# Order of the split products in a two-layer encoder: x low first, and the low weight part right behind the high one for half of each page

## The chip, the cores and the metric

The kernel runs on one core of one Trainium2 chip. The metric is the device time of the whole program in microseconds, the median of several runs. PE is TensorE, DVE is VectorE, ACT is ScalarE, POOL is GpSimd, SP is the engine that issues most loads.

## The reference

Two layers over 256 tokens of width 4096. Each layer normalises x, makes one combined input projection (4096 x 11264), runs an attention branch and a retention branch on its columns, gates both, and adds the output projection (4096 x 4096) of their concatenation to x. A last normalisation follows.

```python
for l in range(DEPTH):                       # 2
    h = rmsnorm(x, norm_w[l])
    proj = h @ w_in[l]                       # (256, 4096) @ (4096, 11264)
    aq, ak, av, ag, rq, rk, rv, rg = jnp.split(proj, SPLIT_POINTS, axis=-1)
    a_out = silu(ag) * gqa_attention(rope(norm(aq)), rope(norm(ak)), av)
    r_out = silu(rg) * rmsnorm(bidirectional_retention(rope(rq), rope(rk), rv), ret_norm[l])
    x = x + concat([a_out, r_out]) @ w_out[l]     # (256, 4096) @ (4096, 4096)
return rmsnorm(x, final_norm)
```

Everything is float32, and nearly all the work lies in the two projections.

## The kernel before

**Blocks and pairs.** Each projection is a phase (four in all: in, out, in, out). A phase runs over blocks of 1024 output columns (11 blocks for the input projection, 4 for the output one), and a block over 16 pairs of 128-row pieces of the inner dimension. For each pair the two halves of the tokens and the two pieces of rows make a 2 x 2 product of blocks, and the kernel computes it by fewer products than the eight of the plain way: seven for the pairs in `SEVEN_IN` or `SEVEN_OUT` (through sums of blocks), eight for the others. Each product adds into one of seven PSUM banks M1 to M7. At the end of a block `combining` adds the banks into two pages of SBUF, `ca` and `cb`.

**Pages.** The weights come as pages of 128 x 1024 (tile `wraw`, six buffers). A page is used by some products, its `uses`: an eight-product pair has two pages of four uses, a seven-product pair has three pages of two uses, two of them sums of weight blocks (`wsum`), and one with a single use (a half page, `whb` and `wlb`).

**High and low parts.** A product of float32 values is made of three matmuls on rounded parts (type fp32r): high weight by high x, high weight by low x, low weight by high x. The x part (128 x 128) is the stationary operand, the weight part (128 x 512) the moving one. The parts of x lie in SBUF for a whole phase (`x7h`, `x7l`, `x8h`, `x8l`, `xmh`, `xml`). The parts of a weight page are made as it comes: ACT casts it to `whi` (four buffers), DVE subtracts for `wlo` (three buffers). For the "far" pages ACT makes both `fhi` and minus `fhi` in `flo`, and a DMA from POOL's queue adds the weights to `flo`. Four pairs (`DIRECT`) of the first block use the plain float32 data (part "D").

**The order of the work around the change.** In `block` (line 1516) a list `units` is written: for each page its "H" units (two matmuls with the high weight) and "L" units (one matmul with the low weight). Before, all H units of a page come first, then all its L units. The pages of the last pair (15) are sorted by bank instead, each use as H and then L. The pages `PAGE_E` of the very last block go to the end (`rest_units`). PE runs the units in exactly this order, each waiting for its data.

**The planner.** While the program is written, `run` (line 851) keeps clocks of PE, ACT and DVE with assumed costs, and hands each engine its next instruction when that clock says it would be free: the weight casts and subtractions (`Weights.high`, `Weights.low`), the splitting of x for the next phase (`split_pair`), and the steps of attention and retention, whose small matmuls (`product`, line 1114, into the bank `ps`) are put between the units. So the orders on ACT, DVE and PE depend on when the planner believes a unit can start. A page's buffers are given back when its last unit has been written (`Weights.release`).

Of the kernel before, what the change touches and what calls it, by code (L numbers as in the profile page):

```python
# [183 lines left out]
def pages_in_order(phase, first=False, last=False):  # L184
    late = [_p for _p in range(NP - 1) if _p not in SEVENS[phase]][-LATE_PAIRS:] if last else []
    skip = DIRECT if first else ()
    order = []
    for _g in groups_of(SEVENS[phase]):
        if _g[0] in skip:
            order += [(_p, _k) for _p in _g for _k in (PAGE_A, PAGE_B)]  # L190
        else:
            order += pages_of([_p for _p in _g], first and _g[0] == 0)
    for _p, _k in order:
        if _p in SEVENS[phase] and _p not in skip:
            yield _p, _k, [(_b, (ALL, _a), _h) for _b, _a, _pg, _h in SEVEN_PRODUCTS if _pg == _k]
        else:
            yield _p, _k, [
                (_b, (_i, _a), _h)
                for _b, _i, _a, _pg, _h in EIGHT_PRODUCTS
                if _pg == _k and not (_p in late and _b == "M4")  # L200
            ]
    for _p in late:
        yield _p, PAGE_E, [("M4", (_i, 1), _i) for _i in range(2)]
# [119 lines left out]
def hybrid_encoder(  # L323
# [43 lines left out]
    def t(pool, shape, tag, bufs=None, dt=F32):  # L367
        kw = {} if bufs is None else {"bufs": bufs}
        return pool.tile(shape, dt, tag=tag, name=tag, **kw)

    def f32(v):
        return v.bitcast(F32)
# [672 lines left out]
    bank = [False, 0.0]  # L1045
# [64 lines left out]
    def matmul(out, a, b, start, stop, passes=1):  # L1110
        nc.tensor.matmul(out, a, b, start=start, stop=stop)  # L1111
        pe.until = max(pe.until, now.t) + MM[math.prod(out.shape[1:])] * passes
# [7 lines left out]
    def at(parts, *index):  # L1120
        return [v[index] for v in parts]
# [391 lines left out]

    bank_at = dict.fromkeys(BANKS, 0.0)

    def block(after_pair, phase, first_order=False, order=LAST_ORDER, last=None):

        phase_now[0] = phase
        units = []
        tail, rest_units = [], []
        for p, k, uses in pages_in_order(phase, first_order, last is not None):
            if k == PAGE_E:
                rest_units += [(p, k, use, "H") for use in uses] + [(p, k, use, "L") for use in uses]
                continue
            if first_order and (p, k) == (DIRECT[0], PAGE_A):  # L1530
                uses = uses[1:] + uses[:1]
            if first_order and p in DIRECT:
                units += [(p, k, use, "D") for use in uses]
                continue
            if p == NP - 1:
                tail += [(p, k, use) for use in uses]
                continue
            units += [(p, k, use, "H") for use in uses] + [(p, k, use, "L") for use in uses]
        tail.sort(key=lambda v: order.index(v[2][0]))
        for v in tail:  # L1540
            units += [v + ("H",), v + ("L",)]
        units += rest_units
        first = {b: next(i for i, v in enumerate(units) if v[2][0] == b) for b in BANKS}
        final = {b: max(i for i, v in enumerate(units) if v[2][0] == b) for b in BANKS}
        left, uses = {}, {}
        for p, k, _, _ in units:
            left[p] = left.get(p, 0) + 1
            uses[p, k] = uses.get((p, k), 0) + 1
        acc, pages, c, fin = {}, {}, Columns(), {}
        done = []  # L1550
        urgent.append(Lane((last or combining)(acc, fin, c, order)))
        for n, (p, k, (bank, index, h), part) in enumerate(units):
            if n == len(units) - COMBINE_LEAD:
                wanted[0] = 2
            while (p, k) not in pages:
                g = weights.pages[weights.at]
                weights.at += 1
                assert g.phase == phase
                pages[g.pair, g.kind] = g
            g = pages[p, k]  # L1560

            def ready():
                if part == "D":
                    return (
                        weights.has(g, "raw")
                        and p in plain
                        and plain[p][2 if index[1] == 2 else 1] <= now.t
                        and (n != first[bank] or bank_at[bank] is not None and bank_at[bank] <= now.t)
                    )
                when = g.high_at if part == "H" else g.low_at  # L1570
                if when is None or not (when() if callable(when) else when <= now.t) or version[p] != phase or operand_at[p] > now.t:
                    return False
                return n != first[bank] or (bank_at[bank] is not None and bank_at[bank] <= now.t)

            yield ready
            if n == first[bank]:
                acc[bank] = t(pm, [P, NB], bank)
                bank_at[bank] = None
            if part == "D":
                a = None  # L1580
            elif g.seven:
                a = at(operand[p], *index, ALL)
            else:
                a = at(operand[p], ALL, 4 + index[0] if index[1] == 2 else 2 * index[0] + index[1], ALL)
            if part == "D":
                matmul(acc[bank], plain[p][0][index], f32(g.raw[0])[:, h], n == first[bank], n == final[bank], 4)
            elif part == "H":
                b = g.hi if k == PAGE_B and g.seven else g.hi[:, h]
                matmul(acc[bank], a[0], b, n == first[bank], False)
                matmul(acc[bank], a[1], b, False, False)  # L1590
            else:
                b = g.lo if k == PAGE_B and g.seven else g.lo[:, h]
                matmul(acc[bank], a[0], b, False, n == final[bank])
            if n == final[bank]:
                fin[bank] = pe.done
            uses[p, k] -= 1
            if not uses[p, k]:
                weights.release(g)
            left[p] -= 1
            if not left[p]:  # L1600
                done.append(p)
                if part == "D":
                    plain_left.remove(p)
            while done and all(not left[q] for q in range(min(done))):
                q = min(done)
                done.remove(q)
                after_pair(q)
        return c
# [181 lines left out]
    def program():  # L1790
        nonlocal sums
        for l, L in enumerate(layers):
            for bi, (one, _) in enumerate(BLOCKS):
                if bi == N_IN - 1:
                    turning.append(Turn(2 * l + 1))
                c = yield from block(turn_over, 2 * l, l == 0 and bi == 0)

                if bi == N_IN - 2:
# [45 lines left out]
            for n in range(N_OUT2):  # L1844
                final = n == N_OUT2 - 1
                if last_layer and final:

                    def after(p):
                        if p == LATE_PAIR:
                            for i in range(2):  # L1850
                                for m in range(MT):
                                    tag = "x8h" if m else "x8l"
                                    r = f32(t(ap, [P, 6, P], tag, EIGHT_ALWAYS, F32R))
                                    rest[i, m] = r[:, :4].rearrange("p k s -> p (k s)")
                                    rest["at"] = dma("sync", rest[i, m], residual(l, N_OUT - 2 + i, m))
                            for i in range(2):
                                r = f32(t(ap, [P, 6, P], ("x8h", "x8l")[i], EIGHT_ALWAYS, F32R))
                                fn.append(r[:, :4].rearrange("p k s -> p (k s)"))
                                dma("sync", fn[i], final_norm[columns(N_OUT - 2 + i)].partition_broadcast(P))

                    yield from block(after, 2 * l + 1, order=FINAL_ORDER, last=last_combining)
                else:
                    if final:
                        turning.append(Turn(2 * l + 2))
                    c = yield from block(turn_over, 2 * l + 1)
                    task(out_tasks(l, n, c), lambda c=c: c.done, need=4, own=2, hurry=n > 1, due=need_at.get((2 * l + 2, 4 * n + 1), 2e9) - DUE_LEAD)
# [70 lines left out]
```

## Time and profile before

| | us |
|---|---|
| three runs | 2621.02, 2621.44, 2623.92 |
| median | 2621.44 |
| the profiled execution's own time | 2623.02 |
| its span | 2621.2 |
| mean granted clock of PE over the span | 0.995 |

Of the span, PE is busy 99%, the loads of its stationary operand 81%, DVE 89%, ACT 73%, POOL 17%. A row of a group in the profile has the line, the engine, the operation, output and inputs by name (so `M<-whi,x8h` is a product into a bank M from the moving `whi` and the stationary `x8h`), the shapes, the count, then busy time and the mean duration of one, then the engine's idle time just before and what ended it. A timeline row has start and duration in us ahead of the same names; `[0.78 <-DVE wlb]` is idle time before it and what ended it. A row of the list of waits reads: who waited for whom, us in total, how many times, the longest one.

### The profile page before, as it was taken

The page shows a single profiled execution, that of the slowest core. Times are in us where ns is not written, and L with a number is a line of the kernel's source. Part 1 is how long each engine was busy: PE and PEld are TensorE (multiplying, and loading weights), DVE is VectorE, ACT ScalarE, POOL GpSimd, SP SyncE. Part 2 cuts the span into 40 slices and gives each one's busy share as a digit, 9 for nine tenths or more (in the row PEclk, how much of TensorE's full clock was granted, in tenths as well). Part 3 has the DMA queues.
Part 4 walks back from the last instruction along what each step waited for, and adds up shares of the span by engine and source line. Part 5 has one row for each costly group of instructions (what it writes and reads, how often), then busy time and mean ns, then how long its engine had stood idle before and what let it go on. Part 6 is the DMA issues. An engine that isn't in the chain of part 4 may idle for free.

```text
span 2621.2 us, 34650 instructions
## 1 busy us (share of the span) xinstructions
PE 2582.6 (99%) x11570; PEld 2124.0 (81%) x11570; DVE 2323.9 (89%) x2908; ACT 1910.0 (73%) x2672; POOL 436.2 (17%) x592
## 2 busy tenths in 40 slices
PE   9999999999999999999999999999999999999997
PEld 5788888888888888788788888888888888877886
DVE  7898988998888889888998889989989888997888
ACT  8777776777767688666877776767768676886665
POOL 0112211221211110221111211212212121101110
PEclk9999999999999999999999999999999999999999
DMA  9999999998898898999999999989989988989997
GB/s 298 309 296 284 273 285 281 272 300 265 279 281 267 282 272 247 296 281 279 309 270 281 287 277 290 276 267 299 282 263 283 279 263 281 283 243 273 268 275 237
DMA packets 214227, 729.62 MB, mean 278 GB/s; under 512 B 25760, under 2 KB 32544, under 8 KB 214048
## 3 DMA queue, kind: packets, MB, share of 16 engines
q1 hardware_dynamic: 149200, 523.44, 56.7%
q0 software_dynamic: 64848, 203.98, 34.3%
q8 instruction: 90, 1.47, 0.2%
q14 instruction: 89, 0.73, 0.1%
HBM read 679.08 MB, written 48.23 MB: 277 GB/s over the span
## 4 chain that ended last, share of the span: by engine, by line
PE 80%; DVE 7%; issue 4%; DMA 4%; ACT 2%; POOL 1%; SPq 0%; DVEq 0%; ACTq 0%; POOLq 0%
PE M L1111 77%; DVE wlo L232 3%; PE ps L1111 3%; DMA wraw<-in_w_in 1%; DVE wsum L232 1%; DMA pT<-p_dram 1%; ACT whi L232 1%; DMA flo<-in_w_in 1%; DVE cb L232 1%; DMA q<-q_dram 0%; DVE ca L232 0%; ACT fhi L232 0%; DMA q_dram<-cb 0%; DVE x8l L232 0%; DVE wlb L232 0%
## 5 line engine op out<-in xcount | busy, mean ns | idle before, releaser
L232 ACT CAST whi<-wraw 128x1024 fp32r<-128x1024 f32 x525 | 547.0, 1048 | 203.8 <-PE M L1111 172.8
L232 DVE TENSOR_TENSOR wlo<-wraw,whi 128x1024 fp32r<-128x1024 f32 x525 | 636.2, 1220 | 51.7 <-ACT whi L232 24.9
L232 DVE TENSOR_TENSOR wlo<-wsum,whi 128x1024 fp32r<-128x1024 f32 x432 | 526.2, 1218 | 116.7 <-PE M L1111 111.7
L232 ACT CAST whi<-wsum 128x1024 fp32r<-128x1024 f32 x432 | 453.2, 1049 | 142.4 <-PE M L1111 125.8
L1111 PE MATMUL M<-whi,x7h 128*128 128x512 f32 x1248 | 487.8, 391 | 0.0
L1111 PE MATMUL M<-whi,x7l 128*128 128x512 f32 x1248 | 486.2, 390 | 0.0
L1111 PE MATMUL M<-whi,x8h 128*128 128x512 f32 x1060 | 415.7, 392 | 6.2 <-DVE ca L232 3.1
L1111 PE MATMUL M<-whi,x8l 128*128 128x512 f32 x1060 | 414.5, 391 | 0.0
L1111 PE MATMUL M<-wlo,x7h 128*128 128x512 f32 x1248 | 386.4, 390 | 0.7 <-DVE wlo L232 0.7
L1111 PE MATMUL M<-fhi,x8h 128*128 128x512 f32 x844 | 328.8, 390 | 0.0
L1111 PE MATMUL M<-fhi,x8l 128*128 128x512 f32 x844 | 328.8, 390 | 0.0
L232 ACT CAST fhi<-wraw 128x1024 fp32r<-128x1024 f32 x215 | 226.0, 1051 | 136.6 <-PE M L1111 103.0
L1111 PE MATMUL M<-wlo,x8h 128*128 128x512 f32 x1060 | 315.9, 394 | 4.3 <-DVE wlo L232 4.1
L348 POOL DMA_DIRECT2D flo<-in_w_in x157 | 140.9, 897 | 1057.1 <-ACT flo L232 969.0
L232 DVE TENSOR_TENSOR wsum<-wraw 128x1024 f32<-128x1024 f32 x216 | 263.1, 1218 | 14.7 <-DMA wraw<-in_w_in 11.9
L1111 PEld LDWEIGHTS M<-whi,x7h 128*128 128x128 f32 x1248 | 234.9, 188 | 48.5 <-issue 0.5
L1111 PEld LDWEIGHTS M<-whi,x7l 128*128 128x128 f32 x1248 | 234.7, 188 | 48.7 <-issue 0.5
L1111 PEld LDWEIGHTS M<-wlo,x7h 128*128 128x128 f32 x1248 | 233.2, 188 | 49.6 <-DVE wlo L232 2.3
L1111 PEld LDWEIGHTS M<-whi,x8h 128*128 128x128 f32 x1060 | 199.9, 189 | 51.3 <-DVE ca L232 6.6
L1111 PEld LDWEIGHTS M<-wlo,x8h 128*128 128x128 f32 x1060 | 200.3, 190 | 48.5 <-DVE wlo L232 7.8
L232 ACT ACTIVATE flo<-fhi 128x1024 fp32r<-128x1024 f32 x215 | 228.3, 1062 | 6.8
L1111 PEld LDWEIGHTS M<-whi,x8l 128*128 128x128 f32 x1060 | 199.9, 189 | 41.0
(257 smaller groups left out, 3762.5 us busy)
## 6 DMA issues: line engine op xcount, KB each, us to landing
wraw<-in_w_in SPq DMA_DIRECT2D x703, 512.0 KB, 5.9
wraw<-in_w_out SPq DMA_DIRECT2D x256, 512.0 KB, 6.1
flo<-in_w_in POOLq DMA_DIRECT2D x157, 512.0 KB, 8.7
flo<-in_w_out POOLq DMA_DIRECT2D x58, 512.0 KB, 8.5
full<-next_dram POOLq DMA_DIRECT2D x18, 512.0 KB, 8.8
p_dram<-room POOLq DMA_DIRECT2D x64, 128.0 KB, 4.2
pT<-p_dram POOLq DMA_DIRECT2D x16, 512.0 KB, 9.1
next_dram<-room POOLq DMA_DIRECT2D x40, 128.0 KB, 6.2
```

The source lines that it names most:

```text
L232: return call(out, *args, **kwargs)
L348: getattr(nc, name).dma_start(to, src, **kw)
L1111: nc.tensor.matmul(out, a, b, start=start, stop=stop)
```

## The change

The list of units of a page is now made by `passes_of`. For the first half of the page's uses all H units come first; then for the second half each use has its H and its L unit next to one another; then the L units of the first half follow, in reverse. With four uses: H0 H1 H2 L2 H3 L3 L1 L0; with two: H0 H1 L1 L0; with one: H L. And in an H unit the matmul with the low part of x now goes first, so that the high part of x is the stationary operand of the last matmul of H and of the L behind it.

```diff
+    def passes_of(p, k, uses):
+
+        n = len(uses) // 2
+        return [(p, k, use, "H") for use in uses[:n]] + [(p, k, use, part) for use in uses[n:] for part in "HL"] + [
+            (p, k, use, "L") for use in uses[:n][::-1]
+        ]
+
...
             if k == PAGE_E:
-                rest_units += [(p, k, use, "H") for use in uses] + [(p, k, use, "L") for use in uses]
+                rest_units += passes_of(p, k, uses)
...
-            units += [(p, k, use, "H") for use in uses] + [(p, k, use, "L") for use in uses]
+            units += passes_of(p, k, uses)
         tail.sort(key=lambda v: order.index(v[2][0]))
-        for v in tail:
-            units += [v + ("H",), v + ("L",)]
+        for p, k, use in tail:
+            units += passes_of(p, k, [use])
...
             elif part == "H":
                 b = g.hi if k == PAGE_B and g.seven else g.hi[:, h]
-                matmul(acc[bank], a[0], b, n == first[bank], False)
-                matmul(acc[bank], a[1], b, False, False)
+                matmul(acc[bank], a[1], b, n == first[bank], False)
+                matmul(acc[bank], a[0], b, False, False)
```

The number of matmuls, their operands and the banks they add into are the same in both kernels; so are the loads, casts and subtractions.

## The prediction

> **What bounds the kernel now.** I read the page's first two parts, then the matmul groups of its fifth part, then a stretch of the timeline, because a busy share says nothing about how densely the matmuls follow one another.
>
> ```profile
> span 2621.2 us, 34650 instructions
> PE 2582.6 (99%) x11570; PEld 2124.0 (81%) x11570; DVE 2323.9 (89%) x2908; ACT 1910.0 (73%) x2672; POOL 436.2 (17%) x592
> ...
> L1111 PE MATMUL M<-whi,x8h 128*128 128x512 f32 x1060 | 415.7, 392 | 6.2 <-DVE ca L232 3.1
> L1111 PE MATMUL M<-wlo,x8h 128*128 128x512 f32 x1060 | 315.9, 394 | 4.3 <-DVE wlo L232 4.1
> ```
>
> PE is the bound, DVE is second. Every matmul record has its own weight-load record (11570 of each). A record of 392 ns is longer than its place in the stream, since records overlap; the distance between starts is what counts. Here are the last products of a block (pair 15), where a use runs high with x high, high with x low, low with x high:
>
> ```profile
> 1566.63 0.39 PE L1111 MATMUL M<-wlo,x8h 128*128 128x512 f32 x1
> 1566.86 0.39 PE L1111 MATMUL M<-whi,x8h 128*128 128x512 f32 x1
> 1567.09 0.39 PE L1111 MATMUL M<-whi,x8l 128*128 128x512 f32 x1
> 1567.31 0.39 PE L1111 MATMUL M<-wlo,x8h 128*128 128x512 f32 x1
> 1567.54 0.39 PE L1111 MATMUL M<-whi,x8h 128*128 128x512 f32 x1
> 1567.77 0.39 PE L1111 MATMUL M<-whi,x8l 128*128 128x512 f32 x1
> ...
> 1567.31 0.39 PE L1111 MATMUL M<-wlo,x8h 128*128 128x512 f32 x1
> 1567.32 0.19 PEld L1111 LDWEIGHTS M<-whi,x8h 128*128 128x128 f32 x1
> 1567.54 0.39 PE L1111 MATMUL M<-whi,x8h 128*128 128x512 f32 x1
> ```
>
> Starts are 0.22 to 0.23 us apart (0.227 on the mean: 1566.63 to 1567.77 is 1.14 us for five), and a load of 0.19 us starts with the matmul before it and is over before its own starts. The changed kernel has 10,776 products of this kind, as before; 10,776 x 0.227 = 2446 us, 93% of the span, is a floor that no order of products changes unless the distance itself changes. What is left for a reordering are the waits of PE:
>
> ```profile
> PE M L1111 <- DVE wlo L232: 4.8, 3, 3.4
> PE ps L1111 <- DVE pTl L232: 3.2, 6, 0.7
> PE M L1111 <- DVE ca L232: 3.1, 5, 1.0
> PE ps L1111 <- DVE aql L232: 2.5, 5, 0.7
> PE M L1111 <- DMA wraw<-in_w_in: 1.9, 1, 1.9
> PE M L1111 <- ACT whi L232: 1.8, 1, 1.8
> PE ps L1873 <- POOL whi L1870: 1.7, 1, 1.7
> PE M L1111 <- DVE wlb L232: 1.6, 3, 0.8
> ...
> PE M L1111 <- DMA flo<-in_w_in: 0.6, 1, 0.6
> PE M L1111 <- DMA flo<-in_w_out: 0.2, 1, 0.2
> ```
>
> These waits are about 20 us together, in some thirty places. So a gain of over 1% can come only from the distance.
>
> **The change, part by part.**
>
> *The same stationary operand twice in a row.* In the instruction orders of the two builds I counted neighbouring products with the very same stationary slice: 29 before, 1,992 after, so 1,963 more. No instruction goes: PE has the same number of matmuls in both. What a repeated operand is worth, this trace shows twice. The 29 pairs are in the rows above: a block's tail goes M3, M5, M4, M2, and the last use of M5 and the first of M4 both take slice 1 of pair 15. That is the step from 1567.31 to 1567.54: a load is issued all the same (1567.32) and the distance is 0.23 us. Over all 29 pairs the median distance is 227 ns, as for the other 10,652. The second place is `product` (line 1114), whose first two matmuls share a stationary operand:
>
> ```profile
> 1947.26 0.28 PE L1111 MATMUL ps<-vh,wTh 128*128 128x256 f32 x1
> 1947.38 0.28 PE L1111 MATMUL ps<-vl,wTh 128*128 128x256 f32 x1
> 1947.50 0.28 PE L1111 MATMUL ps<-vh,wTl 128*128 128x256 f32 x1
> 1947.62 0.28 PE L1111 MATMUL ps<-vh,wTh 128*128 128x256 f32 x1
> ```
>
> wTh to wTh takes 0.12 us, as do wTh to wTl and wTl to the next wTh. Value: 0. The bound on the side of a gain: two widths at 227 and 120 ns make (227 - 120) / 256 = 0.418 ns a column, so 227 - 512 x 0.418 = 13 ns a matmul that do not depend on width. Were all of that saved, 1,963 x 13 ns = 25.5 us. A loss from three accumulations in a row into one bank: the tail rows above already run whi, whi, wlo into one bank at 0.227 us, so 0.
>
> The Trainium skill ("TensorE: Matmul & The Clock Gate", section "Back-to-back issue gap") gives an isolated gap of N/2.4 + 2.5, 216 ns at 512 columns, under the 227 ns of the rows; should a repeated operand reach that gap, an estimate from that page is 1,963 x 11 ns = 22 us less. The 29 pairs do not.
>
> *The low part is needed sooner.* A page with four uses ran eight high matmuls, then four low ones. Now the first low one comes after six: its wlo (250 pages) or flo (210 pages) is needed 2 x 0.227 = 0.454 us sooner. Pages with two uses (H0 H1 L1 L0) and with one need it where they did. If every one of the 460 were just in time, that would cost 209 us. What covers it is the lead of DVE. I took every wlo's end against its first reader; of those 250 pages this is the closest:
>
> ```profile
> 2573.02 1.23 DVE L232 TENSOR_TENSOR wlo<-wraw,whi 128x1024 fp32r<-128x1024 f32 x1 [1.98 <-ACT whi L232]
> ...
> 2574.97 0.84 PE L1111 MATMUL M<-wlo,x8h 128*128 128x512 f32 x3
> ```
>
> It is ready at 2574.25, read at 2574.97: 0.72 us, over 0.454. Cost 0. The flo come by DMA, and the list of waits has two that were late already (0.6 and 0.2 us). Each grows by 0.454: +0.9 us; bounds 0 (both landings move sooner) and 1.8 (four such).
>
> *whi is released one matmul later* (its last reader is the ninth of twelve matmuls, not the eighth): ACT's next cast into that buffer can start 0.227 us later on 250 pages. PE waited for whi once in the whole run (1.8 us, near the start), so the four buffers cover it: 0; without that cover 57 us. *x low first* needs the subtraction's result one matmul sooner, a few times a phase; no wait of PE on x7l or x8l is in the list: 0.
>
> *What the planner makes of it.* It writes out the other engines' orders by its own clock, and the two builds agree but for a few places. SP and POOL keep their order. The attention and retention products stand at the same place among the main ones, except that seven groups come one matmul sooner and a few one or two later. Where a group waits for aql or pTl (11 waits above), sooner is 0.227 us more idle time: +0.4 us, bounds -0.5 and +1.6.
>
> The one place that is really rearranged is the border between the layers, near 1300 us:
>
> ```profile
> 1296.00:1303.00 7.00, 6.88 (x31) 5.36 (x29) 6.89 (x14) 6.97 (x10) 0.88 (x1) 1.00 0.68 223
> 1303.00:1310.00 7.00, 3.23 (x12) 2.06 (x12) 6.93 (x9) 5.39 (x7) 0.00 (x0) 1.00 0.75 218
> 1310.00:1314.00 4.00, 3.75 (x10) 2.98 (x11) 3.96 (x7) 2.14 (x7) 0.87 (x1) 0.57 0.82 219
> ...
> 1303.66 0.50 PE L1111 MATMUL M<-wlb,xmh 128*128 128x512 f32 x1 [0.78 <-DVE wlb L232]
> 1310.25 0.79 PE L1111 MATMUL M<-wlo,x8h 128*128 128x512 f32 x1 [3.36 <-DVE wlo L232]
> ...
> 1302.92 0.68 DVE L232 TENSOR_TENSOR wlb<-wraw,whb 128x512 fp32r<-128x512 f32 x1
> ...
> 1312.45 0.42 DVE L232 TENSOR_TENSOR x7l<-full,x7h 128x256 fp32r<-128x256 f32 x1
> 1312.78 0.82 DVE L232 TENSOR_TENSOR x7l<-xf,x7h 128x640 fp32r<-128x640 f32 x1
> ```
>
> The columns of the first three rows are the stretch, its length, and busy time of PE, PEld, DVE, ACT and POOL, then the granted clock. DVE is busy 6.9 of 7 us there and PE waits for it, so DVE's work counts in full. In the changed order the two x7l subtractions stand ahead of that wlb instead of behind the last wlo: 0.42 + 0.82 = 1.24 us more before both waits. The second wait starts later by what the first grew, so the sum is +1.24 us; bounds -5.8 (0.78 + 3.36 idle and the slow stretch behind them, 4 us at a granted 0.57, so 1.7 us, all gone) and +4 (x7l also waits for ACT's cast, and a second slow stretch follows).
>
> **Sum:** 0 + 0 + 0.9 + 0 + 0.4 + 1.24 = +2.5 us. The profiled execution took 2623.02 us (span 2621.2 and 1.8 around it) and would take 2625.5; the median of the three runs is 2621.44, 1.6 below it, so the forecast is 2624.0 us. That is +0.1%: a measurement of this kernel can tell about 0.2% (5.2 us) from no change, so I call it the same, 2616.2 to 2626.7.
>
> **The rivals.**
>
> *A repeated operand shortens the stream* (faster). The 13 ns fall away on 1,963 products: 2621.4 - 25.5 + 2.5 = 2598 us. For it: the change makes just such pairs, and 256-wide products are a thin likeness. Against it: the 29 pairs at full width, each with its own load. The Trainium skill says in the same page ("What happens when you issue a matmul") that a stationary operand may be loaded once and used repeatedly; here each matmul loads its own. Chance 0.10.
>
> *Low parts come late* (slower). Place: the 210 far pages, whose flo lands by DMA, and DVE-bound borders like the one above. Price 0.454 us a page; with the +1.6 from the other terms it decides from 8 late pages on (5.2 us). With 15 it is 6.8 + 1.6 = 8.4 us: 2630 us. For it: two flo were late already. Against it: only two of 215. Chance 0.24.
>
> *The border loses its waits*: -5.8 + 1.3 = -4.5 us, 2617 us, since ACT's and DVE's split work is spread otherwise. For it: the orders of ACT and DVE differ in many places there, and the waits are DVE's. Against it: x7l moves the wrong way. Chance 0.08, half of it below 2616.2.
>
> **Numbers.** The forecast has 0.58, of which 0.04 lies above 2626.7. Faster: 0.10 + 0.04 = 0.14. Slower: 0.24 + 0.04 = 0.28. Same: 0.54 + 0.04 = 0.58. The range runs from 2615 (the border gain, a little beyond) to 2633 (some 20 late pages): it leaves out the first rival and the far end of the second, under 2 in 10.
>
> **What would show it.** Right: the steps whi,x8h to wlo,x8h stand 0.227 us apart in the timeline, PEld has 11570 loads again, and PE's waits total a few us more, with wlb near 1304 us waiting about 2 us. Wrong: distances of 0.22 us or less at the repeated operand, or fewer loads; waits of PE on wlo or flo of some 0.4 us in many places.

## The result and the profile after

| | us |
|---|---|
| changed kernel, median of 22 runs | 2626.17 (2620.71 to 2630.55) |
| kernel before, median of 22 runs beside them | 2620.21 (2612.48 to 2624.30) |
| ratio, with its 95% interval | 1.0018 [1.001, 1.0025] |
| the profiled execution of the changed kernel | 2626.18, span 2624.4 |

By the ratio, 0.18% of 2620 us, the changed kernel takes 4.7 us longer (the means differ by 4.9 us, the medians by 6.0). That is on the edge of the 0.2% that the prediction called "the same"; the forecast was 2624.0 and the sum behind it +2.5 us. The profiled execution took 3.2 us longer than that of before (2626.18 against 2623.02).

The first rows of the page of the changed kernel, and one row of its groups:

```profile
span 2624.4 us, 34648 instructions
PE 2581.7 (98%) x11570; PEld 2123.6 (81%) x11570; DVE 2325.8 (89%) x2908; ACT 1911.0 (73%) x2672; POOL 437.2 (17%) x592
...
L1111 PE MATMUL M<-flo,x8h 128*128 128x512 f32 x844 | 262.9, 390 | 2.1 <-DMA flo<-in_w_out 1.1 <-DMA flo<-in_w_in 1.0
```

The bound is the same, and every matmul still has its own load: 11570 of each. PE is busy 0.9 us less than before and the span is 3.2 us longer, so what came in is idle time of PE or lies behind its last matmul. The list of PE's waits in the changed kernel (waiter, what it waited for, us in total, times, longest):

```profile
PE M L1111 <- DVE wlo L232: 5.4, 4, 3.3
PE ps L1111 <- DVE pTl L232: 4.0, 7, 0.9
PE ps L1111 <- DVE aql L232: 2.9, 4, 1.1
...
PE M L1111 <- DMA flo<-in_w_out: 1.1, 1, 1.1
PE M L1111 <- DMA flo<-in_w_in: 1.0, 1, 1.0
```

Over the whole list PE waited 26.1 us in 32 places, before 23.4 us in 31. The two waits for `flo` went from 0.8 to 2.1 us, those for `pTl` and `aql` from 5.7 to 6.9, those for `wlo` from 4.8 to 5.4; all others together went from 12.1 to 11.7.

The rest of the time is at the end. Here are the last rows of before that matter, from its timeline (SPq is the issue of a DMA on SP's queue):

```profile
2601.57 0.39 PE L1111 MATMUL M<-whi,x8h 128*128 128x512 f32 x1
...
2604.00 0.68 DVE L232 TENSOR_TENSOR cb<-cb,M 128x512 f32<-128x512 f32 x1
...
2604.14 0.73 PE L1111 MATMUL M<-wlo,x8h 128*128 128x512 f32 x2
...
2604.60 1.22 DVE L232 TENSOR_TENSOR wlo<-wraw,whi 128x1024 fp32r<-128x1024 f32 x1
...
2605.87 0.73 PE L1111 MATMUL M<-wlo,x8h 128*128 128x512 f32 x2
...
2607.51 0.34 SPq L348 DMA_DIRECT2D out<-ca  x1
```

The same place in the changed kernel:

```profile
2603.61 0.39 PE L1111 MATMUL M<-whi,x8l 128*128 128x512 f32 x1
...
2606.07 1.22 DVE L232 TENSOR_TENSOR wlo<-wraw,whi 128x1024 fp32r<-128x1024 f32 x1
...
2607.20 0.68 DVE L232 TENSOR_TENSOR cb<-cb,M 128x512 f32<-128x512 f32 x1
...
2607.34 0.73 PE L1111 MATMUL M<-wlo,x8h 128*128 128x512 f32 x2
...
2610.52 0.34 SPq L348 DMA_DIRECT2D out<-ca  x1
```

Before, DVE added bank M3 into `cb` and then made the last `wlo`. In the changed kernel the last `wlo` comes ahead of that addition. The addition is what the final normalisation of the first half of the tokens waits for, so the first output is issued 4.45 us after the start of the last `wlo` (2610.52 - 2606.07), not 2.91 (2607.51 - 2604.60). From the start of the last matmul (the second of the pair in the row, 2606.21 before and 2607.68 after) to the end of the span it is 15.03 us before and 16.69 after: +1.67 us. The stream ahead of it grew by 1.47 us in these two executions.

The +1.67 us is not all price, though, since the last matmul itself waits for the last `wlo`. Before, PE lost 0.30 us at 2604.14 and 0.25 us at 2605.87 to `wlo`, against starts 0.227 us apart; in the changed kernel it lost 0.10 us, at 2607.34, because each `wlo` is made one addition sooner. Counted from an earlier matmul that both kernels have at the same place (the eighteenth from the end, the first row of either block above), the first output is issued 5.94 us later before and 6.91 after: +0.97 us. The remaining 0.13 us lies between the first output and the end of the span (13.72 and 13.85 us).

### The profile page after: what moved, and what is told of

Read it like the earlier page. It is cut to its first block, busy times and chain, and to the rows that moved or that the text cites. A ratio compares the mean times of both kernels' runs of the same rounds, so it can differ in the third digit from the quotient of the medians.

```text
span 2624.4 us, 34648 instructions
## 1 busy us (share of the span) xinstructions
PE 2581.7 (98%) x11570; PEld 2123.6 (81%) x11570; DVE 2325.8 (89%) x2908; ACT 1911.0 (73%) x2672; POOL 437.2 (17%) x592
## 3 DMA queue, kind: packets, MB, share of 16 engines
q8 instruction: 90, 1.47, 0.2%
## 4 chain that ended last, share of the span: by engine, by line
PE 84%; DVE 6%; DMA 5%; issue 3%; ACT 1%; POOL 1%; SPq 0%; DVEq 0%; POOLq 0%; ACTq 0%
PE M L1111 80%; PE ps L1111 3%; DVE wlo L232 3%; DMA pT<-p_dram 1%; DVE wsum L232 1%; DMA flo<-in_w_out 1%; DMA wraw<-in_w_out 1%; DMA wraw<-in_w_in 1%; DMA q<-q_dram 1%; DVE cb L232 0%; ACT whi L232 0%; DVE pTl L232 0%; DMA flo<-in_w_in 0%; DVE wlb L232 0%; POOL rq_dram L348 0%
## 5 line engine op out<-in xcount | busy, mean ns | idle before, releaser
L1111 PE MATMUL M<-wlo,x8h 128*128 128x512 f32 x1060 | 348.6, 393 | 3.9 <-DVE wlo L232 3.9
L1111 PE MATMUL M<-flo,x8h 128*128 128x512 f32 x844 | 262.9, 390 | 2.1 <-DMA flo<-in_w_out 1.1
```

## The experiments

Each ratio is against the kernel before, run beside it on the same chip, with its 95% interval; n is the number of runs. "Ending" is the time from the start of the last matmul to the end of the span in the profiled execution; it contains the shift of the last matmul just described, so a new order in the last block shows there with some 1.5 us where its price is 1.0. Profiled executions of one program differ by several us in the stream, so sizes of the stream are read from the timed runs and not from one profile.

**The changed kernel once more.** No edit.

> The changed kernel once more, as the yardstick for the others on this chip. Both theories: +0.1 to +0.25% against the kernel before (+3 to +6 us); its profile again has matmul starts 0.227 us apart at a repeated stationary operand, and the last matmul starts about 16.5 us before the end of the span (15.0 before the change).

Measured: 2627.73 us (n = 7), ratio 1.0027 [1.0016, 1.0037], ending 16.69. The difference is real, and the ending repeats to 0.01 us.

**x low first, alone.** In the kernel before only the two matmuls of an H unit change places:

```diff
-                matmul(acc[bank], a[0], b, n == first[bank], False)
-                matmul(acc[bank], a[1], b, False, False)
+                matmul(acc[bank], a[1], b, n == first[bank], False)
+                matmul(acc[bank], a[0], b, False, False)
```

> Kernel before, and only the two matmuls of an H unit are swapped (x low first); units, and with them the orders of ACT, DVE, POOL and SP, are those of before. My theory (the order of a use's matmuls costs nothing by itself; the 29 pairs with a repeated operand that before has are gone): no change, within 0.1% (2.6 us). Rival (x low parts are read 0.227 us sooner and come late, or a repeated operand is worth something): slower by 0.1% or more, with waits of PE on x7l or x8l.

Measured: 2620.80 us (n = 11), ratio 0.9998 [0.9989, 1.0007], ending 15.03. This part shows no cost; the interval reaches from -2.9 to +1.8 us. The list of waits has none on `x7l` or `x8l`.

**The new order of units without the repeated operand.** The changed kernel with x high first again, so that the L unit no longer follows a matmul with its own stationary operand:

```diff
-                matmul(acc[bank], a[1], b, n == first[bank], False)
-                matmul(acc[bank], a[0], b, False, False)
+                matmul(acc[bank], a[0], b, n == first[bank], False)
+                matmul(acc[bank], a[1], b, False, False)
```

> The changed kernel, but with x high first in an H unit, as before. The low product then follows a matmul with x low, so nearly none of the 1,992 pairs with a repeated stationary operand are left, while the orders of ACT, DVE, POOL and SP are those of the changed kernel to the instruction. My theory (a repeated operand is worth nothing, the order of the units and what the planner makes of it is all): the same time as the changed kernel within 0.1%, so +0.1 to +0.25% against before. Rival (the repeated operand saves something that the waits take back): slower than the changed kernel, by 1,963 x 2.6 ns = 5 us at 2.6 ns a pair.

Measured: 2625.17 us (n = 11), ratio 1.0011 [1.0001, 1.0021], ending 16.70. Without the pairs the kernel is not slower than with them (1.0018 and 1.0027), so the pairs bring nothing that the runs can see.

**The old order in the very last block alone.** In the changed kernel `passes_of` gives all H and then all L where `last is not None`:

```diff
-        n = len(uses) // 2
+        n = len(uses) if keep_order[0] else len(uses) // 2
...
-            (p, k, use, "L") for use in uses[:n][::-1]
+            (p, k, use, "L") for use in (uses if keep_order[0] else uses[:n][::-1])
...
+        keep_order[0] = last is not None
```

> The changed kernel, with the old order of units in the very last block alone. In the changed kernel the last subtraction for a low part stands ahead of the addition of bank M3 on DVE, here behind it as before. My theory (1.7 us of the 3.1 us between the two profiles arise after the last matmul, because the first half's ending starts later): the last matmul starts about 15.0 us before the end of the span again instead of 16.7, and the time is 1.5 us (0.06%) less than the changed kernel. Rival (the ending is set by the last matmul and output transfers alone, the 1.7 us are chance): 16.5 us stay.

Measured: 2621.50 us (n = 12), ratio 1.0002 [0.9991, 1.0012], ending 15.16. The same kernel again, since the answer was closer to no difference than the ending allows for:

> The changed kernel with the old order in the last block, timed again, since its first interval (0.9991 to 1.0012) left the split between ending and stream open. My theory: +0.05 to +0.15% against before (the stream's part), with 15.1 us behind the last matmul. Rival (the last block is all of it): within 0.05% of before.

Measured: 2625.04 us (n = 12), ratio 1.0024 [1.0007, 1.004], ending 15.17. One program gave 1.0002 and 1.0024 in two series of twelve: that is how far such a series can be off. What is certain here is the ending, 15.16 and 15.17: the order in the last block sets it. The first output is issued 10.92 and 10.93 us after the fortieth-last matmul, as before (10.93), and 11.90 us after it in the changed kernel.

**The reverse: the new order in the last block alone**, x low first everywhere.

```diff
-        keep_order[0] = last is not None
+        keep_order[0] = last is None
```

> The old order of units in all blocks but the very last, which has the new one (x low first throughout, which cost nothing by itself). Only in the last block do the orders of PE and DVE differ from before: one subtraction for a low part ahead of the addition of bank M3. My theory (this alone makes the ending 1.67 us longer; the rest of the measured 4 to 6 us arises in the stream): 16.7 us between the last matmul's start and the end of the span, and +0.06% against before (+1.7 us). Rival (the last block carries nearly all of the loss, since putting its old order back gave 1.0002): +0.15 to +0.25%.

Measured: 2622.58 us (n = 12), ratio 1.0009 [0.9997, 1.0022], ending 16.56. The ending comes with the last block, and so does the later first output (11.90 us after the fortieth-last matmul, +0.97). The time agrees with such a price, but its interval holds no change too.

**All uses as H and L**, not only the second half of a page (about 3,590 repeated operands):

```diff
-        n = len(uses) // 2
+        n = 0
```

> Every use has its high and low unit next to one another, on all pages, with x low first: some 3,590 pairs with a repeated stationary operand instead of 1,992. A page with four uses now needs its low part six matmuls (1.36 us) sooner than before, one with two uses two matmuls (0.45 us) sooner; the planner writes a rather different order. My theory (a repeated operand is worth nothing, a low part needed sooner costs only where the lead was less): starts 0.227 us apart at the repeated operand, PE's waits on wlo and flo grow by 2 to 8 us, and the time is +0.1 to +0.5% against before. Rival (each repeated operand is worth some ns that waits hid before): faster than the changed kernel.

Measured: 2657.93 us (n = 4), ratio 1.0146 [1.0124, 1.0168], ending 14.72. The size was missed by far. The list of waits, 50.5 us in all against 23.4 before, says where most of it went:

```profile
PE M L1111 <- DVE x7l L232: 18.2, 2, 9.1
PE M L1111 <- DVE wlo L232: 11.7, 19, 2.4
```

Two waits of 9 us at the start of a phase (near 1044 and 2365 us), where DVE makes `x7l` later than PE wants it. That is not the price of a pair: DVE's order, written anew by the planner, has other work ahead of `x7l` there, and the distance at a repeated operand is 227 ns again. The 19 waits on `wlo` (4 in the changed kernel) go with a low part asked for still sooner, though no run holds the plan fixed here.

**Another plan with the old order.** How much does it cost if the planner merely decides otherwise? One assumed cost of the planner in the kernel before:

```diff
-PE_PASS = 0.2
+PE_PASS = 0.17
```

> Control: kernel before with its units untouched; only the planner's assumed time for a result of PE to be seen is 0.17 instead of 0.20 us (PE_PASS), which rearranges some 120 lines of DVE's order and moves some attention products. My theory (the stream's part of the loss is what any rearrangement of the planned orders may bring, of either sign): between -0.15% and +0.15%, not zero for sure. Rival (rearranging alone costs nothing, the new order of the products does): within 0.03% of before.

Measured: 2622.04 us (n = 12), ratio 1.0009 [1.0, 1.0019], ending 15.12. So another plan may cost about 2 us (by the means +1.7, standard error 0.8), but the interval begins at no change, and the rival's 0.03% lies within it.

**The new order of matmuls under the old plan.** The orders of ACT, DVE, POOL and SP are those of the kernel before, to the instruction; only PE's matmuls within a page stand in the new order, with x low first, where the page's low part has been made in time by the plan (1,922 pairs; pages with the last unit of a bank keep the old order):

```diff
+            if count == 4:
+                swapped[key] = [low[2], high[3], low[3], low[1], low[0]]
+                swap_at[key] = high[3]
+            else:
+                swapped[key] = [low[1], low[0]]
+                swap_at[key] = low[0]
...
+                if swap_at[p, k] == n and may_swap(g, spans[p, k]):
+                    queue[p, k] = [v for u in swapped[p, k] for v in parts_at(u)]
```

> New order of the products, old plan: ACT, DVE, POOL and SP run exactly the orders of the kernel before, and only PE's matmuls within a page stand in the new order, with x low first (1,922 of the pairs with a repeated operand; first low product after six matmuls on all four-use pages). My theory (the loss in the stream, some 3 us, comes from what the planner rearranged, not from low parts needed sooner): within 0.07% of before (2 us), ending 15.0 us as before. Rival (low parts are needed 0.45 us sooner on 460 pages, flo above all): +0.1% or more, with more of PE's waits on flo and wlo.

Measured: 2622.66 us (n = 12), ratio 1.0016 [1.0006, 1.0026], ending 15.17. My theory at that point, that the order itself costs nothing and all of it comes from the plan and the ending, fell: with plan and ending of before the order alone is slower. Its one profile doesn't show where: that execution was a short one (2619.01 us), and PE's waits in it are 23.8 us in all, against 23.4 before.

**The old order of matmuls under the new plan.** The mirror: the orders of the other engines are those of the changed kernel, PE runs its matmuls in the old order with x high first, except in the last block.

```diff
+            if count == 4:
+                swapped[key] = [high[3]] + low
+                swap_at[key] = low[2]
+            else:
+                swapped[key] = low
+                swap_at[key] = low[1]
```

> The converse: the changed kernel's plan (orders of ACT, DVE, POOL and SP to the instruction, its last block included), but in all blocks but the last PE's matmuls within a page stand in the old order with x high first (the first page that opens banks excepted). My theory: the changed kernel's time, +0.12 to +0.25% against before, 16.7 us behind the last matmul. Rival: only the ending's 1.7 us are left, +0.03 to +0.1%.

Measured: 2623.27 us (n = 11), ratio 1.0018 [1.001, 1.0027], ending 16.68. It has the new ending, at a price of 1.0 us; the rest, some 3 us (means: +3.9 us with a standard error of 1.1, less 1.0), is within the errors of what another plan cost above.

**The far pages.** The kernel of the old plan again, but pages whose `flo` comes by DMA keep the old order:

```diff
-            return g.low_at is not None
+            return g.low_at is not None and not g.far
```

> The kernel with the new order of products and the old plan (it measured 1.0016), but the far pages (fhi and flo, whose low part lands by DMA) keep the old order of their units. My theory now (the order costs by flo being needed sooner: PE's waits on flo were 1.7 to 3.9 us in six profiles with the new order on far pages and 0.4 to 1.4 us in six without): waits on flo back at 0.3 to 1.4 us, and the time within 0.1% of before, nearer to it than 1.0016. Rival (the order of the other pages costs, or the whole difference is the scatter between groups of runs): 1.001 to 1.0025 again, with flo's waits small all the same.

Measured: 2617.57 us (n = 12), ratio 0.9989 [0.998, 0.9999]. The interval does not touch that of the kernel without this edit, [1.0006, 1.0026]; the means of the two, each against its own runs of before on its own chip, are +3.5 and -1.9 us, a difference of 5.4 with a standard error of 1.7. The waits for `flo` differ in the same sense. The kernel with the new order on far pages has two lines for `flo`:

```profile
PE M L1111 <- DMA flo<-in_w_out: 1.5, 2, 1.1
...
PE M L1111 <- DMA flo<-in_w_in: 0.5, 1, 0.5
```

The one with the old order there has none; these are its longest waits:

```profile
PE M L1111 <- DVE wlo L232: 6.2, 5, 3.4
PE ps L1111 <- DVE pTl L232: 3.0, 5, 0.9
PE ps L1111 <- DVE aql L232: 2.4, 3, 0.9
```

Over the other profiles it is the same. With the new order on the far pages PE waited for `flo` 2.1, 3.8, 1.9, 1.7, 3.9 and 2.0 us (2.6 on the mean); with the old order there 0.8, 0.4, 1.3, 0.5, 1.4, 0.6 and 0 (0.7); all uses as H and L had 3.1. So the far pages carry a cost, and its visible part is 1.9 us. That they carry the whole difference of 5.4 isn't shown: two series of one and the same program were 6.0 us apart above (+0.2 and +6.2), and the whole list of waits is 25.1 us in this kernel's profile, more than the 23.8 of the kernel with the new order on far pages.

As a kernel this one is not clearly better than the one before: 0.1% under it, with an interval that ends at 0.9999, less than a measurement of this kernel can tell.

**The ending.** If DVE's order at the end costs 1 us, can one win there? The kernel before, edited so that the sums of both halves (M4's addition and the second half's squares with it) come ahead of the first half's scaling and outputs:

```diff
-                yield from finish(0 if b == "M3" else 1, c)
+                yield from finish_sums(0 if b == "M3" else 1, c)
+        finish_rows()
```

> Kernel before with another ending: the addition of the last bank (M4) and the sums of squares of the second half stand ahead of the first half's scaling and output, instead of behind them. Units and all that comes before stand as in before. My theory (the ending is a chain on DVE: what stands ahead of the second half's addition delays the end): 1 to 3 us less behind the last matmul than 15.0, and 0.05 to 0.1% faster than before. Rival (the output transfers of SP's queue set the end, with 16 of some 0.5 us each): 15.0 us stay, or more.

Measured: 2621.78 us (n = 11), ratio 1.001 [1.0001, 1.0018], ending 16.93. The theory behind it fell (by the means the kernel is 2.3 us slower, with a standard error of 0.7), and its profile says what does set the end. Timeline rows of this kernel:

```profile
2606.11 0.34 SPq L348 DMA_DIRECT2D out<-ca  x1
...
2615.50 0.56 SPq L348 DMA_DIRECT2D out<-cb  x1
```

All sixteen outputs are issued in one run without the pause that the kernel before has between its halves, and still the span ends 13.6 us after the first of them (2619.71 - 2606.11). Before it is 13.7 (2621.24 - 2607.51), after 13.9 (2624.38 - 2610.52), and over all profiles it lies between 13.60 and 13.89. The DMA view of the last 20 us, from 2605 on, in slices of half a microsecond; first the kernel before, then this one:

```profile
GB/s 0 0 0 0 0 0 98 385 389 377 369 389 381 373 389 381 369 291 254 385 385 385 381 377 385 385 373 389 385 131 0 0 0 0 0 0 0 0 0 0
DMA packets 2305, 4.20 MB, mean 210 GB/s; under 512 B 256, under 2 KB 256, under 8 KB 2304
```

```profile
GB/s 0 0 0 29 385 381 377 377 381 381 381 385 381 369 381 393 389 373 381 385 393 373 397 373 377 356 8 0 0 0 0 0 0 0 0 0 0 0 0 0
DMA packets 2305, 4.20 MB, mean 210 GB/s; under 512 B 256, under 2 KB 256, under 8 KB 2304
```

The outputs are 4.20 MB, and at some 380 GB/s they need 11 us, with the pause or without; before, only two of the 22 slices between the first and the last fall short (291 and 254). So the end hangs on when the first output is issued: 1.3 us after the start of the last matmul before, 2.84 in the changed kernel, 3.3 here (the start of the last matmul being 2602.78, the second of its pair). PE's order is that of before here, so the 2.03 us between 1.3 and 3.3 are all price; in the changed kernel 0.97 of the 1.54 are. What is put ahead of the first output is not made up for later.

## Why the prediction was right, step by step, and where it was not

*The repeated stationary operand: 0, right.* The tail of the block that the prediction showed, in the timeline of the changed kernel:

```profile
1568.28 0.39 PE L1111 MATMUL M<-whi,x8l 128*128 128x512 f32 x1
1568.51 0.39 PE L1111 MATMUL M<-whi,x8h 128*128 128x512 f32 x1
1568.74 0.39 PE L1111 MATMUL M<-wlo,x8h 128*128 128x512 f32 x1
1568.96 0.39 PE L1111 MATMUL M<-whi,x8l 128*128 128x512 f32 x1
```

From `whi,x8h` to `wlo,x8h`, one operand twice, 0.23 us, as to the next. Over the whole trace the median distance is 227 ns for the 1,992 such pairs and 227 ns for the other 8,690 distances. The first rival (2598 us) is refuted by this and by the run without pairs. The Trainium skill ("TensorE: Matmul & The Clock Gate", section "Back-to-back issue gap") gives an isolated gap of 216 ns at 512 columns; this trace doesn't agree, at 227 ns in either case.

*Low part sooner, `wlo`: 0, right.* PE's waits on `wlo` are 5.4 us against 4.8; the largest, 3.34 against 3.36, is that of the border. Over the profiles they are 4.7 to 6.0 us in the five of the changed order and plan and 4.8 to 5.5 in the four with units and plan as before, the very last block aside: no difference.

*Low part sooner, `flo`: +0.9, mis-sized.* This is the term of the sum that was too small. The prediction let the two late landings grow by 0.454 us each. One did: near 1397 us it went from 0.61 to 0.97. The other late one is a new place. Timeline of the changed kernel:

```profile
1398.33 0.50 PE L1111 MATMUL M<-flo,x8h 128*128 128x512 f32 x1 [0.97 <-DMA flo<-in_w_in]
...
2280.45 0.50 PE L1111 MATMUL M<-flo,x8h 128*128 128x512 f32 x1 [1.06 <-DMA flo<-in_w_out]
```

That place is late by more than the 0.454 us explains: its transfer took 9.9 us from issue to landing before and 11.2 us after. So what the term had wrong is that a landing stays where it was and only the need moves. One profile's two late ones were too few to count with: the mean over the profiles is 1.9 us more waiting, at the upper bound of 1.8. The second rival had the place right (far pages, `flo`), but not the number: of more than 200 far pages it is always some of the same six that are late (near 980, 1250, 1397, 1430, 2280 and 2590 us; all uses as H and L left aside), never 15.

A late landing can cost more than its wait. In three profiles with the new order and plan the page near 1430 us was 1.6 to 3.1 us late, and in two of these the granted clock was 0.50 right behind the wait. Here it is in the profile of the changed kernel once more, first PE's wait, then the stretch behind it (the last three columns are granted clock, DMA share and GB/s):

```profile
1430.50 0.56 PE L1111 MATMUL M<-flo,x8h 128*128 128x512 f32 x1 [2.04 <-DMA flo<-in_w_in]
...
1430.80:1434.20 3.40, 3.40 (x9) 2.64 (x8) 2.67 (x5) 1.97 (x2) 0.00 (x0) 0.50 0.85 304
```

By these figures I estimate 1.7 us more, half of 3.4; in the other profile (a wait of 3.11 us, then 5.8 us at 0.50) 2.9. On the mean of the six profiles this adds 0.8 us to the 1.9. Whether the runs of the new order under the old plan, +3.5 us (standard error 1.1), are made up so stays open: in their one profile the page near 1430 us was in time, so its lateness may be the new plan's.

*x low first: 0, right* within the -2.9 to +1.8 us of the run of it alone (0.9998).

*The attention and retention products: +0.4, bounds -0.5 and +1.6.* In these two profiles the waits for `pTl` and `aql` grew by 1.2 us together, within the bounds. Over the profiles they grew by more: 3.6 to 7.1 us in the five of the changed order and plan (6.1 on the mean), 2.7 to 5.7 in the six with the old plan (3.9). That is +2.1 with a standard error of 0.8: two standard errors over the +0.4, less than one over the upper bound.

*The layers' border: +1.24, right in kind.* The order there in the changed kernel, DVE and PE:

```profile
1302.82 0.42 DVE L232 TENSOR_TENSOR x7l<-full,x7h 128x256 fp32r<-128x256 f32 x1
...
1303.16 0.82 DVE L232 TENSOR_TENSOR x7l<-xf,x7h 128x640 fp32r<-128x640 f32 x1
1303.89 0.68 DVE L232 TENSOR_TENSOR wlb<-wraw,whb 128x512 fp32r<-128x512 f32 x1
...
1304.63 0.50 PE L1111 MATMUL M<-wlb,xmh 128*128 128x512 f32 x1 [0.79 <-DVE wlb L232]
...
1311.22 0.50 PE L1111 MATMUL M<-wlo,x8h 128*128 128x512 f32 x1 [3.34 <-DVE wlo L232]
```

As forecast, both `x7l` stand ahead of `wlb`, and both waits end 0.97 us later (1304.63 for 1303.66, 1311.22 for 1310.25). What I had wrong is that `wlb`'s wait would grow to 2 us: it stayed at 0.79, since PE came as late to it. PE came to the border 0.30 us behind the old time already, by what earlier places had added; the border's own share, a new wait of 0.31 us on ACT's `whb` with it, is some 0.65 us. The third rival (the border loses its waits) did not happen.

*The ending: no term at all, +1.0.* This is the step that the prediction left out. It wrote that the other engines' orders agree "but for a few places" and priced one of them. Another is the very end, where the last three `wlo` moved ahead of an addition each on DVE, the last of them ahead of M3's. There nothing runs behind that could hide it: the outputs wait. From the fortieth-last matmul to the first output it was 10.92 or 10.93 us in all seven profiles with DVE's old order in the last block and 11.89 or 11.90 in all five with the new one, so this part is shown. (The ending as counted from the last matmul was 15.03 to 15.17 and 16.56 to 16.70.)

*The sum.* The order under the old plan costs +3.5 us (standard error 1.1) and the ending +1.0, together 4.5; the changed kernel's means are +4.9 (1.0) and +6.6 (1.3) in its two series. The new plan apart from the ending had about +3 us in the run that has it alone, but the changed kernel with the old last block, +0.2 (1.3) and +6.2 (2.0), leaves room for that or for nothing. The lists of waits give another account. PE waited 25.0 to 29.2 us in the five profiles of the changed order and plan (26.4 on the mean) and 22.0 to 23.4 in the four with units and plan as before (22.7): +3.7, which `flo` and the attention products make up, and with the ending +4.7. With order or plan alone it was 23.8 and 24.0, each in one profile. So what grew is seen, but how it splits between order and plan is not known to the last microsecond.

That the time came out "the same" and not slower was partly luck. With the ending, the forecast's own sum would have been +3.5, and with the waits as the profiles have them in place of its terms +4.7; the median of 2626.17 lies half a microsecond under the bound of 2626.7, and the second series, at 2627.73 us and 1.0027, lies beyond it.

## What to carry to other kernels

Interleaving products so that neighbours share a stationary operand was worth nothing here, where each matmul loads its own operand and the load is hidden: look first whether the distance of two starts differs at such a pair in the trace at hand. What the reordering does cost is lead time: an operand that arrives by DMA has a spread of landings, so look over several profiles which landings come close to their need, not how many were late in one. And compare the instruction orders at the very end with most care: one subtraction of 1.22 us that slipped ahead of the first output there showed with 0.97 us. When such a price is counted, count it from a point that the change does not move.

## What the runs showed of the hardware

The output is a stretch of fixed length: 4.20 MB went out at some 380 GB/s in about 11 us, and the span ended 13.6 to 13.9 us after the first issue, whether the sixteen issues came in one run or with a pause. I had not expected the output to be the bound of the ending. And landings of one and the same DMA vary by enough that a program with the same instruction order waits for `flo` 2.1 us in one execution and 3.8 in another, in different places. The far page near 1430 us landed between 9.6 and 17.1 us after its issue over the profiles.
